# Pinning the transfers between two matrix products, and the last operand splits, to text order

## The chip, the cores and the metric

The kernel runs on one core of a Trainium2 chip. The metric is the device time of one execution in microseconds (us), the median of several runs. The engines named here are TensorE (PE, with its weight loads PEld), VectorE (DVE), ScalarE (ACT), GpSimd (POOL) and SyncE (SP), which here only issues DMA transfers; SPq is its queue.

## The reference

One layer of a streaming encoder, 1024 tokens of width 1024, float32. Only its end matters here:

```
x = x + concat(mixers) @ W_out                  # 1024 x 1024
h = rms_norm(x, mlp_norm_g)
f = square(relu(h @ W1))                        # 1024 -> 4096
x = x + f @ W2                                  # 4096 -> 1024
```

## The kernel before, in words

Every product is computed with operands split into a high part (rounded to the fast fp32r format) and a low remainder, so a product takes three matmuls (`mm3`): high x high, high x low, low x high. A split costs a cast on ACT and a subtraction on DVE. Weights are split by `w_split` into `whi` and `wlo`.

The two MLP products (FF1 with W1, FF2 with W2) are each done by a seven-product scheme on 2x2 blocks: instead of eight block products there are seven, numbered 1 to 7, on sums and differences of blocks. Those sums are made by POOL (`left`, `right`) and, for the activations x of FF1, in `x2_ready`. The work is a list of **units** of 12 matmuls of 128x512: ("1", p, i) is FF1, column block p (0 to 15), product i; ("2", c, i, n) is FF2, chunk c of p's, product i, n-th p of the chunk. `mlp(n)` issues the transfers of unit n, prepares (splits) the operands of unit n+2 and runs unit n. FF1's products are stored to DRAM by `f_store` as `f{p}_{i}` (seven tiles of 256 KB for each p) and read back by `load_f` for FF2. FF2's weights come by `load_w2` (two tiles of 512 KB for each p). The residual x, saved to `x2d` in DRAM by `x2_ready`, is loaded again (eight tiles of 512 KB) into slots that FF1 has finished with.

`x2_ready(dt)` runs behind the last output-projection matmuls of row block dt. It stores x2[dt] to DRAM, squares it for the norm, scales it in place by the norm weight on ACT, and makes the splits for products 1 and 5 (dt < 4) or 6, 2 and part of 7 (dt >= 4); `x2_late` then makes the rest of 7, and 4 and 3, in one go. Tiles of splits: P4 to P7 are product 6, P8 to P11 product 2, P12, P13, xh3, xl3 product 7, P0 to P3 product 4, xh0, xl0, P16, P17 product 3.

The order on each engine is not that of the text: a scheduler at build time sorts instructions by its own estimate of when their inputs are there. So a transfer whose slot is free early can go ahead of one that stands earlier in the text. Instructions of one engine then run in that order, each waiting for its inputs, and all DMA issues named here are in SP's one queue.

Of the kernel before, what the change touches and what calls it, by code (L numbers as in the profile page):

```python
# [29 lines left out]
V_MIX, V_MLP, V_GQ, V_GK, V_RET, V_PWA, V_PWG = 0, 8, 16, 17, 18, 22, 24  # L30
# [46 lines left out]
def build(tc, d):  # L77
    nc = tc.nc
# [8 lines left out]
    V, S, GP, TE = nc.vector, nc.scalar, nc.gpsimd, nc.tensor  # L87
    uid = [0]

    def nm(s):  # L90
        uid[0] += 1
        return f"{s}_{uid[0]}"

    def bank(tag):
        return pp.tile([P, 512], F32, tag=tag, name=nm(tag))

    def slot(tag, shape=(P, T), dt=F32):
        pool = xp if tag[0] == "x" else pg
# [57 lines left out]
    vec = cp.tile([P, V_N], F32, tag="vec", name="vec")  # L156
# [543 lines left out]
    x2, x2d = [], []  # L700
    for dt in range(NK):
        t = slot(X2S[dt])
# [12 lines left out]
          3: ("xh0", "xl0", "P16", "P17")}  # L715
    xr = {}

    def x_split(i, kk, src):
        t = slot(XS[i][kk], (P, 2, 512), F32R)
        S.copy(t[:, 0, :], src)  # L720
        V.tensor_tensor(out=t[:, 1, :], in0=src, in1=t[:, 0, :].bitcast(F32), op=ALU.subtract)
        xr[i, kk] = t

    sq2 = {}

    def x2_ready(dt):
        x = x2[dt]
        nc.sync.dma_start(x2d[dt], x)
        if dt == 0:
            sq = sq2[0] = pg.tile([P, T], F32, tag="glu0", name="sq2")  # L730
        else:
            sq = slot(("DM", "glu1")[dt % 2])
        S.activation(sq, x, AF.Square)
        S.activation(x, x, AF.Copy, scale=vec[:, V_MLP + dt:V_MLP + dt + 1])
        kk = dt % 4
        a, b = x[:, 0:512], x[:, 512:1024]
        if dt < 4:
            x_split(1, kk, a)
            GP.tensor_tensor(out=a, in0=b, in1=a, op=ALU.subtract)
            x_split(5, kk, a)  # L740
        else:
            t, b12 = x2[kk][:, 0:512], x2[kk][:, 512:1024]
            V.tensor_tensor(out=t, in0=b, in1=t, op=ALU.subtract)
            x_split(6, kk, t)
            x_split(2, kk, a)
            GP.tensor_tensor(out=b12, in0=b, in1=b12, op=ALU.subtract)
            if kk < 2:
                x_split(7, kk, b12)
            GP.tensor_tensor(out=t, in0=a, in1=t, op=ALU.subtract)
        if dt > 0:  # L750
            V.tensor_tensor(out=sq2[0], in0=sq2[0], in1=sq, op=ALU.add)

    def x2_late():
        for kk in range(2, 4):
            x_split(7, kk, x2[kk][:, 512:1024])
        for kk in range(4):
            x_split(4, kk, x2[kk][:, 0:512])
        for kk in range(4):
            x_split(3, kk, x2[kk + 4][:, 512:1024])
# [74 lines left out]

    def f_store(p, i, src):
        fd[p, i] = dp.tile([P, 512], F32, tag=f"f{p}_{i}", name=f"f{p}_{i}")
        nc.sync.dma_start(fd[p, i], src)

    def hidden(o, src, hf):
        V.scalar_tensor_tensor(out=o, in0=src, scalar=0.0, in1=rbc2[:, 512 * hf:512 * hf + 512], op0=ALU.max,  # L840
# [74 lines left out]
    def load_w2(p):  # L915
        raw2[p] = []
        for j in range(2):
            tag = WS2[nw2[0]]
            nw2[0] += 1
            t = wp.tile([P, 1024], F32, tag="wr", name=nm("wr"), bufs=4) if tag == "wr" else slot(tag)  # L920
            nc.sync.dma_start(t, d["w_ff2"][2 * p + j])
            raw2[p].append(t)

    fin = {}
# [1 line left out]
    def load_f(p, i):  # L926
        t = slot(FI[nfi[0] % len(FI)], (P, 512))
        nfi[0] += 1
        nc.sync.dma_start(t, fd[p, i])
        fin[p, i] = t  # L930

    def r_split(src):
# [20 lines left out]
    def run_ff2(c, i, n):  # L953
        s = {1: "X", 6: "X", 7: "X", 4: "X", 5: "Y", 3: "Y", 2: "Y"}[i]
        first = i in (1, 5, 2)
        if n == 0 and first:
            ps2[s] = [bank(t) for t in {"X": "ggtt", "Y": "zzoo"}[s]]
        wh, wl = opl.pop((c, i, n))
        fh, fl = opr.pop((c, i, n))
        last = n == len(chunks[c]) - 1  # L960
        for dt in range(4):
            cs = slice(dt * P, dt * P + P)
            mm3(ps2[s][dt], wh[:, cs], wl[:, cs], fh, fl, first and n == 0, last, not first)
        if not last:
            return
        rh, ch = {1: (0, 0), 2: (0, 0), 5: (1, 1), 7: (1, 1), 6: (0, 1), 3: (0, 1), 4: (1, 0)}[i]
        for dt in range(4):
            a = x2[4 * rh + dt][:, 512 * ch:512 * ch + 512]
            add(a, ps2[s][dt], a)
            if c == len(chunks) - 1 and i in (3, 7, 2, 4):  # L970
                r = (4 * rh + dt) * P
                nc.sync.dma_start(d["yT"][r:r + P, 512 * ch:512 * ch + 512], a)

    order1 = (1, 5, 6, 2, 7, 4, 3)
    units = [("1", 0, 1), ("1", 0, 5), ("1", 1, 1), ("1", 1, 5)]
# [2 lines left out]
    n1 = len(units)  # L978
# [8 lines left out]
    def f_upto(n):  # L987
        while nf[0] < min(n, len(f_order)):
            load_f(*f_order[nf[0]])
            nf[0] += 1  # L990

    def transfers(n):

        v = units[n + 2] if n + 2 < len(units) else None
        if v and v[0] == "1" and v[2] == 6 and v[1] + 2 < npair:
            load_w1(v[1] + 2)
        if n == n1 - 7:
            load_w2(0)
            load_w2(1)
            f_upto(3)  # L1000
        if n == n1 - 5:
            for dt in range(NK):
                x2[dt] = slot(C[dt])
                nc.sync.dma_start(x2[dt], x2d[dt])
        if n == n1 - 4:
            load_w2(2)
            f_upto(4)
        if n == n1 - 2:
            f_upto(6)
        if n >= n1:  # L1010
# [10 lines left out]
    def mlp(n):  # L1021
        transfers(n)
        if n + 2 < len(units):
            prep[units[n + 2][0]](*units[n + 2][1:])
        run[units[n][0]](*units[n][1:])

    for dt in range(NK):
# [49 lines left out]
```

## Time and profile before

| | |
|---|---|
| median of 3 runs | 1180.6 us (1180.12 to 1184.6) |
| profiled execution | 1179.3 us, of which the span of the profile is 1177.4 us |
| PE busy | 1131.6 us (96% of the span) |
| DVE, POOL, ACT busy | 867.1, 541.9, 489.8 us |

PE is busy nearly all the time, so what can be won lies in the few places where it stands still or runs at a lower clock. The page's second part gives 40 slices of 29.4 us each: the output projection ends and FF1 begins in slice 18 (counted from 0), FF2 begins in slices 28 and 29.

### The profile page before, as it was taken

The numbers are of one execution on the slowest core, as the hardware profiler recorded it, in microseconds if no ns is written. First come the engines' busy times: TensorE is split into PE (matmuls) and PEld (weight loads), VectorE is DVE, ScalarE is ACT, GpSimd is POOL, SyncE is SP. The second block draws the span as 40 slices with busy tenths as digits, with TensorE's granted clock in tenths as the row PEclk, the third lists the DMA queues.
The fourth block names the chain that finished last, engine by engine and source line by source line (L and its number), as shares of the span: only waits on it lengthen the run. The fifth ranks groups of instructions, "written<-read, shape, count | busy, mean of one in ns | idle before, by whom it ended". The sixth has DMA issues, their size and how long they took to land.

```text
span 1177.4 us, 17628 instructions
## 1 busy us (share of the span) xinstructions
PE 1131.6 (96%) x6376; PEld 984.6 (84%) x6376; DVE 867.1 (74%) x1347; ACT 489.8 (42%) x925; POOL 541.9 (46%) x440
## 2 busy tenths in 40 slices
PE   7999999999999999997999999999669999999998
PEld 6998889999999998786888888888458888888887
DVE  6787766769897887689765657574749797896964
ACT  7675644532323243555433333333324434444441
POOL 3565545346752553354555565647553250531400
PEclk9999999999999999998999999999889999999999
DMA  8111111021111151213444444453995346233332
GB/s 283 37 37 37 54 41 48 22 63 60 55 60 38 53 189 54 78 57 117 161 143 143 161 147 160 145 166 126 370 352 168 101 140 191 81 108 89 108 123 93
DMA packets 63734, 137.11 MB, mean 116 GB/s; under 512 B 7200, under 2 KB 11936, under 8 KB 63648
## 3 DMA queue, kind: packets, MB, share of 16 engines
q1 hardware_dynamic: 63072, 135.56, 35.0%
q8 instruction: 50, 0.82, 0.3%
q10 hardware_dynamic: 576, 0.44, 0.1%
q14 instruction: 36, 0.29, 0.1%
HBM read 98.22 MB, written 37.75 MB: 115 GB/s over the span
## 4 chain that ended last, share of the span: by engine, by line
PE 73%; DVE 12%; DMA 6%; issue 4%; POOL 2%; ACT 2%; SPq 0%; DVEq 0%; ACTq 0%; POOLq 0%
PE g L108 12%; PE g L110 11%; PE g L109 11%; PE t L108 4%; PE t L110 4%; PE t L109 4%; PE z L109 3%; PE z L110 3%; PE z L108 3%; PE o L108 3%; PE o L109 3%; PE o L110 3%; DVE wlo L153 3%; PE o L366 2%; PE t L347 1%
## 5 line engine op out<-in xcount | busy, mean ns | idle before, releaser
L153 DVE TENSOR_TENSOR wlo<-sum,whi 128x512 fp32r<-128x512 f32 x78 | 78.9, 1011 | 95.0 <-ACT whi L152 91.2
L153 POOL TENSOR_TENSOR wlo<-wraw,whi 128x512 fp32r<-128x512 f32 x57 | 86.2, 1527 | 78.0 <-ACT whi L152 75.5
L152 ACT CAST whi<-sum 128x512 fp32r<-128x512 f32 x78 | 48.1, 618 | 115.2 <-POOL sum L810 50.9
L153 DVE TENSOR_TENSOR wlo<-wr,whi 128x512 fp32r<-128x512 f32 x80 | 79.0, 993 | 12.1 <-ACT whi L152 12.1
L336 POOL TENSOR_TENSOR be<-be,kp 128x512 f32<-128x512 f32 (+3 forms) x48 | 46.0, 961 | 78.4 <-DVE kp L332 49.9
L152 ACT CAST whi<-wr 128x512 fp32r<-128x512 f32 x80 | 48.2, 619 | 56.0 <-PE g L109 16.8
L815 POOL TENSOR_TENSOR sum<-wr 128x512 f32<-128x512 f32 x16 | 24.5, 1529 | 101.5 <-DMA wr<-in_w_ff_dram 79.3
L152 ACT CAST whi<-wraw 128x512 fp32r<-128x512 f32 x68 | 41.8, 621 | 58.0 <-DMA wraw<-in_w_in_dram 21.8
L332 DVE TENSOR_TENSOR_SCAN kp<-kp 128x512 f32<-128x512 f32 (+3 forms) x48 | 51.1, 1066 | 10.6 <-ACT kp L325 10.1
L525 DVE SCALAR_TENSOR_TENSOR DM__508_2651<-glu,vec,DM__508_2651 128x512 f32<-128x512 f32 x60 | 53.9, 937 | 0.1
L167 POOL TENSOR_TENSOR rs<-ss,nhalf 128x4 f32<-128x4 f32 (+1 forms) x36 | 37.3, 1038 | 30.2 <-DVE ss L633 15.3
L525 DVE SCALAR_TENSOR_TENSOR glu<-glu,vec 128x512 f32<-128x512 f32 x60 | 47.5, 854 | 0.0
L810 POOL TENSOR_TENSOR sum<-wr,sum 128x512 f32<-128x512 f32 x19 | 32.0, 1684 | 7.5 <-DVE wlo L153 7.5
L325 ACT ACTIVATE kp<-z 128x512 f32<-128x512 f32 (+3 forms) x48 | 23.6, 494 | 16.7 <-PE z L322 13.0
L108 PE MATMUL g<-whi,xh__12_100 128*128 128x256 f32 x82 | 25.3, 309 | 2.8 <-DVE P__107_556 L300 0.9
L810 POOL TENSOR_TENSOR sum<-sum,wr 128x512 f32<-128x512 f32 x18 | 25.2, 1402 | 3.0 <-DVE wlo L153 3.0
L326 ACT ACTIVATE be<-z 128x512 f32<-128x512 f32 (+3 forms) x48 | 23.4, 493 | 4.9 <-PE t L347 4.9
L108 PE MATMUL g<-whi,xh__34_250 128*128 128x256 f32 x82 | 23.4, 285 | 1.7 <-ACT xh__34_250 L186 1.7
L110 PE MATMUL g<-whi,xl__53_362 128*128 128x256 f32 x82 | 23.3, 286 | 1.6 <-DVE xl__53_362 L187 1.6
L347 PE MATMUL t<-ident,be 128*128 128x128 f32 x144 | 24.2, 274 | 0.1
L110 PE MATMUL g<-whi,xl__46_323 128*128 128x256 f32 x82 | 23.4, 287 | 0.4 <-DVE xl__46_323 L187 0.4
L109 PE MATMUL g<-wlo,xh__52_361 128*128 128x256 f32 x82 | 23.5, 287 | 0.0
(2892 smaller groups left out, 4366.6 us busy)
## 6 DMA issues: line engine op xcount, KB each, us to landing
wr<-in_w_ff_dram SPq DMA_DIRECT2D x40, 512.0 KB, 3.9
wraw<-in_w_in_dram SPq DMA_DIRECT2D x52, 256.0 KB, 3.1
P__418_2109<-in_rot_dram SPq DMA_DIRECT2D x32, 128.0 KB, 2.1
wraw<-in_w_out_dram SPq DMA_DIRECT2D x16, 256.0 KB, 2.7
P__18_143<-in_xT_dram SPq DMA_DIRECT2D x1, 512.0 KB, 4.7
P__22_176<-in_xT_dram SPq DMA_DIRECT2D x1, 512.0 KB, 5.7
P__29_215<-in_xT_dram SPq DMA_DIRECT2D x1, 512.0 KB, 3.7
P__33_248<-in_xT_dram SPq DMA_DIRECT2D x1, 512.0 KB, 7.3
```

What stands on the lines that cost most here:

```text
L108: TE.matmul(out, lh, rh, start=start, stop=False, skip_group_check=on)
L109: TE.matmul(out, lh, rl, start=False, stop=False, skip_group_check=on)
L110: TE.matmul(out, ll, rh, start=False, stop=stop, skip_group_check=on)
L152: S.copy(hi, raw)
L153: (lo_engine or GP).tensor_tensor(out=lo, in0=raw, in1=hi.bitcast(F32), op=ALU.subtract)
L167: GP.tensor_tensor(out=out, in0=in_, in1=nhalf[:, 0:in_.shape[1]], op=ALU.pow)
L332: V.tensor_tensor_scan(rev, rev, rev, kp[:, n:n + 1], op0=ALU.mult, op1=ALU.bypass)
L336: GP.tensor_tensor(out=be[:, 0:n], in0=be[:, 0:n], in1=kp[:, 1:n + 1], op=ALU.mult)
L347: TE.transpose(pt[:, j * P:j * P + P], be[:, j * P:j * P + P], ident)
L525: V.scalar_tensor_tensor(out=acc, in0=src, scalar=vec[:, o:o + 1], in1=acc, op0=ALU.mult, op1=ALU.add)
L810: (eng or GP).tensor_tensor(out=o, in0=x, in1=y, op=ALU.subtract)
L815: GP.tensor_tensor(out=s, in0=a21, in1=a22, op=ALU.add)
```

## The change

Three parts. (1) From unit n1-7 on (n1 is the number of FF1 units; n1-7 is p = 15, product 1) every transfer of the MLP goes through `load`, which pins the DMA behind the instruction that stands before it in the text on SP's queue. The loads of x2 are done in two halves. (2) `x2_late` is cut in three: the rest of product 7 ahead of unit 4, product 4 ahead of unit 5, product 3 ahead of unit 6, each instruction pinned behind its engine's previous one in the text. (3) For dt >= 4 the norm weight g is no longer applied to x in place on ACT: it is folded into the splits (ACT's scale; a scalar_tensor_tensor on DVE), and eight subtractions move from POOL to DVE as scalar_tensor_tensor.

```
+    ordered = [False]
+    def load(out, in_):
+        i = nc.sync.dma_start(out, in_)
+        if ordered[0]:
+            tc.keep_in_program_order(i)
...
+    def x_split(i, kk, src, g=None, late=False):
         t = slot(XS[i][kk], (P, 2, 512), F32R)
...
+            ops = (S.activation(hi, src, AF.Copy, scale=g),
+                   V.scalar_tensor_tensor(out=lo, in0=src, scalar=g, in1=hi.bitcast(F32), op0=ALU.mult,
+                                          op1=ALU.subtract))
+        if late:
+            for o in ops:
+                tc.keep_in_program_order(o)
...
-        S.activation(sq, x, AF.Square)
-        S.activation(x, x, AF.Copy, scale=vec[:, V_MLP + dt:V_MLP + dt + 1])
...
         else:
-            V.tensor_tensor(out=t, in0=b, in1=t, op=ALU.subtract)
+            V.scalar_tensor_tensor(out=t, in0=b, scalar=g, in1=t, op0=ALU.mult, op1=ALU.subtract)
             x_split(6, kk, t)
-            x_split(2, kk, a)
-            GP.tensor_tensor(out=b12, in0=b, in1=b12, op=ALU.subtract)
+            x_split(2, kk, a, g)
+            V.scalar_tensor_tensor(out=b12, in0=b, scalar=g, in1=b12, op0=ALU.mult, op1=ALU.subtract)
             if kk < 2:
                 x_split(7, kk, b12)
-            GP.tensor_tensor(out=t, in0=a, in1=t, op=ALU.subtract)
+            S.activation(sq, x, AF.Square)
...
         if n == n1 - 7:
+            ordered[0] = True
             load_w2(0)
             load_w2(1)
             f_upto(3)
-        if n == n1 - 5:
-            for dt in range(NK):
+        if n in (n1 - 5, n1 - 3):
+            for dt in range(4) if n == n1 - 5 else range(4, NK):
                 x2[dt] = slot(C[dt])
-                nc.sync.dma_start(x2[dt], x2d[dt])
+                load(x2[dt], x2d[dt])
...
-    x2_late()
     for n in range(3, len(units)):
+        if n in (4, 5, 6):
+            x2_late({4: 7, 5: 4, 6: 3}[n])
```

What the built programs say, first on SP where FF2's transfers begin. Before, the stores of p = 14 and 15, the loads of f and the weights of FF2 for p = 4 to 9 (P12 on) stand mixed:

```order
L837 DMA f14_5_8722<-xh5__1450_8595 128x512
L921 DMA P0__1616_9390<-in_w_ff2_dram 128x1024
L837 DMA f14_7_8728<-xl5__1451_8596 128x512
L929 DMA xh4__1474_8741<-f0_1_6468 128x512
L837 DMA f15_1_8919<-xh6__1481_8767 128x512
L837 DMA f14_6_8725<-xh5__1450_8595 128x512
L921 DMA P12__1576_9195<-in_w_ff2_dram 128x1024
L921 DMA P1__1617_9392<-in_w_ff2_dram 128x1024
L837 DMA f14_4_8731<-xl5__1451_8596 128x512
L929 DMA xl4__1475_8743<-f1_1_6587 128x512
L921 DMA P13__1577_9197<-in_w_ff2_dram 128x1024
L921 DMA xh3__1594_9290<-in_w_ff2_dram 128x1024
```

In the changed program the last store of p = 14 comes first, then the weights of p = 0 and 1 (wr, wr, glu0, DM), then the f tiles of FF2's first three units, then half of x2:

```order
L101 DMA f14_4_8727<-xl5__1451_8592 128x512
L101 DMA wr_1470_8729<-in_w_ff2_dram 128x1024
L101 DMA wr_1471_8731<-in_w_ff2_dram 128x1024
L101 DMA glu0__1472_8733<-in_w_ff2_dram 128x1024
L101 DMA DM__1473_8735<-in_w_ff2_dram 128x1024
L101 DMA xh4__1474_8737<-f0_1_6464 128x512
L101 DMA xl4__1475_8739<-f1_1_6583 128x512
L101 DMA xh5__1476_8741<-f2_1_6747 128x512
L101 DMA xh1__1488_8784<-x2d0_5212 128x1024
L101 DMA xl1__1489_8786<-x2d1_5215 128x1024
L101 DMA xh2__1490_8788<-x2d2_5218 128x1024
L101 DMA xl2__1491_8790<-x2d3_5221 128x1024
```

Before the change the weights of p = 0 and 1 stood among the stores of p = 13 or further up, and x2 stood 14 to 24 rows ahead of f14_4, so both had been asked for by then. The next rows now are P4, P5 (weights of p = 2), f0_5, the other half of x2, f1_5, f2_5, the seven stores of p = 15 and f0_6, f1_6, f2_6.

A little further on SP. Before, nine weight tiles that FF2 needs only from chunk 1 on stand between the second (f1_1) and the third f tile (f2_1); these are the last seven of them, three stores and f2_1:

```order
L921 DMA xl3__1595_9292<-in_w_ff2_dram 128x1024
L921 DMA P2__1652_9557<-in_w_ff2_dram 128x1024
L921 DMA P3__1653_9559<-in_w_ff2_dram 128x1024
L921 DMA xh0__1676_9659<-in_w_ff2_dram 128x1024
L921 DMA xl0__1677_9661<-in_w_ff2_dram 128x1024
L921 DMA P16__1694_9755<-in_w_ff2_dram 128x1024
L921 DMA P17__1695_9757<-in_w_ff2_dram 128x1024
L837 DMA f15_3_8921<-xl6__1482_8768 128x512
L837 DMA f15_2_8923<-xl6__1482_8768 128x512
L837 DMA f15_5_8926<-xh7__1483_8769 128x512
L929 DMA xh5__1476_8745<-f2_1_6751 128x512
```

Now the same weight tiles stand one pair at a time between f loads, behind f2_2, f3_1 and so on:

```order
L101 DMA xl6__1557_9093<-f2_2_6751 128x512
L101 DMA wr_1558_9095<-in_w_ff2_dram 128x1024
L101 DMA wr_1559_9097<-in_w_ff2_dram 128x1024
L101 DMA xh7__1563_9119<-f0_4_6480 128x512
L101 DMA xl7__1567_9141<-f1_4_6599 128x512
L101 DMA xh4__1571_9167<-f2_4_6763 128x512
L101 DMA xl4__1575_9189<-f3_1_6911 128x512
L101 DMA P12__1576_9191<-in_w_ff2_dram 128x1024
L101 DMA P13__1577_9193<-in_w_ff2_dram 128x1024
```

So fourteen weight tiles that stood ahead of f0_6 before now stand behind it.

Last, DVE at the start of FF1. Before, six low-part subtractions of products 3 and 4 (xl0, xh0, P16, P1, P0, P2) stand ahead of the weights `wlo_1089` of unit ("1", 1, 6):

```order
L721 TENSOR_TENSOR xl0__1066_6316<-xl6__831_5225,xl0__1066_6316 128x512
L721 TENSOR_TENSOR xh0__1065_6313<-xh6__830_5222,xh0__1065_6313 128x512
L774 TENSOR_TENSOR xl7__833_5231<-o_1045_6236,xl7__833_5231 128x512
L721 TENSOR_TENSOR P16__1067_6319<-xh7__832_5228,P16__1067_6319 128x512
L721 TENSOR_TENSOR P1__1062_6304<-xl4__827_5213,P1__1062_6304 128x512
L721 TENSOR_TENSOR P0__1061_6301<-xh4__826_5210,P0__1061_6301 128x512
L153 TENSOR_TENSOR wlo_1084_6402<-sum1_1012_6060,whi_1083_6401 128x512
L721 TENSOR_TENSOR P2__1063_6307<-xh5__828_5216,P2__1063_6307 128x512
L153 TENSOR_TENSOR wlo_1089_6430<-sum1_1025_6125,whi_1088_6429 128x512
```

Now, from the last output tile (xl7, the residual add of the last row block) on:

```order
L795 TENSOR_TENSOR xl7__833_5231<-o_1045_6230,xl7__833_5231 128x512
L734 SCALAR_TENSOR_TENSOR xl0__1080_6387<-xl6__831_5225,vec_75,xl0__1080_6387 128x512
L734 SCALAR_TENSOR_TENSOR P16__1081_6390<-xh7__832_5228,vec_75,P16__1081_6390 128x512
L761 SCALAR_TENSOR_TENSOR xl5__829_5219<-xl7__833_5231,vec_75,xl5__829_5219 128x512
L764 SCALAR_TENSOR_TENSOR xl5__829_5219<-xl7__833_5231,vec_75,xl5__829_5219 128x512
L161 TENSOR_TENSOR wlo_1084_6398<-sum1_1012_6058,whi_1083_6397 128x512
L769 TENSOR_TENSOR sq2_5831<-sq2_5831,glu1__1046_6248 128x1024
L734 SCALAR_TENSOR_TENSOR P17__1082_6393<-xl7__833_5231,vec_75,P17__1082_6393 128x512
L161 TENSOR_TENSOR wlo_1089_6426<-sum1_1025_6121,whi_1088_6425 128x512
L731 TENSOR_TENSOR P7__1047_6250<-xl5__829_5219,P7__1047_6250 128x512
L731 TENSOR_TENSOR xl3__1063_6307<-xl5__829_5219,xl3__1063_6307 128x512
```

Product 4's work on DVE has moved behind `wlo_1089` (its first instruction stands sixteen rows behind xl7), and two scalar_tensor_tensor on xl5 stand where P0, P1 and P2 stood.

## Rows read from the trace of the kernel before

**Rows 1.** The page, parts 1 and 2: PE busy, granted clock, traffic by slice.
```profile
PE 1131.6 (96%) x6376; PEld 984.6 (84%) x6376; DVE 867.1 (74%) x1347; ACT 489.8 (42%) x925; POOL 541.9 (46%) x440
PE   7999999999999999997999999999669999999998
PEclk9999999999999999998999999999889999999999
```
**Rows 2.** Waits of PE, the longest: who was waited for, us in total, times, longest.
```profile
PE g L108 <- ACT P__1512_8878 L935: 8.8, 1, 8.8
```
**Rows 3.** Timeline of PE, start of FF1: start, duration, [idle before, releaser].
```profile
533.61 0.39 PE L110 MATMUL o<-P__963_5772,wlo 128*128 128x512 f32 x1
...
540.56 0.50 PE L108 MATMUL t<-P__1009_6048,whi 128*128 128x512 f32 x1 [1.12 <-ACT whi L152]
...
546.73 0.80 PE L110 MATMUL t<-P__1009_6048,wlo 128*128 128x512 f32 x1 [5.43 <-DVE wlo L153]
547.32 0.63 PE L108 MATMUL t<-P__1022_6113,whi 128*128 128x512 f32 x1
547.75 0.63 PE L109 MATMUL t<-P__1022_6113,whi 128*128 128x512 f32 x1
```
**Rows 4.** Timeline of DVE, the same stretch.
```profile
541.45 1.75 DVE L721 TENSOR_TENSOR P__1062_6304<-xl__827_5213,P__1062_6304 128x512 fp32r<-128x512 f32 x1
543.12 1.74 DVE L721 TENSOR_TENSOR P__1061_6301<-xh__826_5210,P__1061_6301 128x512 fp32r<-128x512 f32 x1
...
546.00 0.68 DVE L153 TENSOR_TENSOR wlo<-sum,whi 128x512 fp32r<-128x512 f32 x1
```
**Rows 5.** Timeline of POOL: FF1's start, and the last tile of p = 14.
```profile
541.12 1.53 POOL L815 TENSOR_TENSOR sum<-wr 128x512 f32<-128x512 f32 x1 [2.54 <-DMA wr<-in_w_ff_dram]
...
838.63 1.29 POOL L810 TENSOR_TENSOR xl__1451_8596<-xl__1449_8594,xh__1450_8595 128x512 f32<-128x512 f32 x1
```
**Rows 6.** Timeline of ACT: the scaling of x2[7] in place.
```profile
544.25 1.15 ACT L734 ACTIVATE xl__833_5231<-xl__833_5231,vec 128x1024 f32<-128x1024 f32 x1 [2.23 <-DMA x2d<-xl__833_5231]
```
**Rows 7.** One scalar_tensor_tensor form on DVE: duration in ns, min/median/max.
```profile
L840 DVE SCALAR_TENSOR_TENSOR xl__1115_6630<-xl__1115_6630,rbc x2: 676/676/676, 596.8 to 597.4; 128x512 f32<-128x512 f32 x2
```
**Rows 8.** Timeline of PE: FF1's end, then FF2's units 1, 2, 3, 7, 8.
```profile
844.99 0.39 PE L110 MATMUL z<-P__1068_6322,wlo 128*128 128x512 f32 x1
854.13 1.22 PE L108 MATMUL g<-P__1512_8878,whi 128*128 128x512 f32 x2 [8.76 <-ACT P__1512_8878 L935]
...
860.41 0.73 PE L108 MATMUL g<-P__1516_8901,whi 128*128 128x512 f32 x2 [1.58 <-ACT P__1516_8901 L935]
...
870.81 1.22 PE L108 MATMUL g<-P__1525_8953,whi 128*128 128x512 f32 x2 [6.24 <-ACT P__1525_8953 L935]
...
883.69 0.39 PE L108 MATMUL g<-P__1552_9056,whi 128*128 128x512 f32 x1
...
886.41 0.39 PE L108 MATMUL g<-P__1556_9078,whi 128*128 128x512 f32 x1
```
**Rows 9.** Stretches of 5 us: busy of PE, PEld, DVE, ACT, POOL; PEclk, DMA share, GB/s.
```profile
840.00:845.00 5.00, 3.40 (x16) 2.50 (x14) 2.65 (x5) 1.33 (x3) 0.00 (x0) 1.00 1.02 417
...
850.00:855.00 5.00, 0.87 (x2) 0.77 (x3) 3.79 (x5) 1.77 (x3) 4.37 (x4) 0.50 1.04 417
...
865.00:870.00 5.00, 0.00 (x0) 0.00 (x0) 1.29 (x2) 0.57 (x2) 1.64 (x1) 0.80 1.04 402
```
**Rows 10.** Timeline of SP's queue: the issues of f0_1, f14_4, f2_1, f0_5.
```profile
843.64 0.32 SPq L929 DMA_DIRECT2D xh__1474_8741<-f  x1
...
848.60 0.33 SPq L837 DMA_DIRECT2D f<-xl__1451_8596  x1
...
862.51 0.32 SPq L929 DMA_DIRECT2D xh__1476_8745<-f  x1
...
868.94 0.32 SPq L929 DMA_DIRECT2D xl__1502_8828<-f  x1
```
**Rows 11.** DMA issues of one kind: count, KB each, median us to landing.
```profile
wr<-in_w_ff_dram SPq DMA_DIRECT2D x40, 512.0 KB, 3.9
```

More of the change, by code (lines that the diff above doesn't have):

```diff
@@ L716, in build @@
     xr = {}
-    def x_split(i, kk, src):
+    def x_split(i, kk, src, g=None, late=False):
         t = slot(XS[i][kk], (P, 2, 512), F32R)
-        S.copy(t[:, 0, :], src)
-        V.tensor_tensor(out=t[:, 1, :], in0=src, in1=t[:, 0, :].bitcast(F32), op=ALU.subtract)
+        hi, lo = t[:, 0, :], t[:, 1, :]
+        if g is None:
+            ops = S.copy(hi, src), V.tensor_tensor(out=lo, in0=src, in1=hi.bitcast(F32), op=ALU.subtract)
+        else:
+            ops = (S.activation(hi, src, AF.Copy, scale=g),
[4 more added lines that the diff above has]
+                tc.keep_in_program_order(o)
         xr[i, kk] = t
     sq2 = {}
+    gs = [vec[:, V_MLP + dt:V_MLP + dt + 1] for dt in range(NK)]
     def x2_ready(dt):
-        x = x2[dt]
+        x, g = x2[dt], gs[dt]
         nc.sync.dma_start(x2d[dt], x)
@@ L737, in x2_ready @@
         if dt < 4:
+            S.activation(sq, x, AF.Square)
+            S.activation(x, x, AF.Copy, scale=g)
             x_split(1, kk, a)
@@ L742, in x2_ready, with x2_late @@
             t, b12 = x2[kk][:, 0:512], x2[kk][:, 512:1024]
-            V.tensor_tensor(out=t, in0=b, in1=t, op=ALU.subtract)
+            V.scalar_tensor_tensor(out=t, in0=b, scalar=g, in1=t, op0=ALU.mult, op1=ALU.subtract)
             x_split(6, kk, t)
-            x_split(2, kk, a)
-            GP.tensor_tensor(out=b12, in0=b, in1=b12, op=ALU.subtract)
+            x_split(2, kk, a, g)
+            V.scalar_tensor_tensor(out=b12, in0=b, scalar=g, in1=b12, op0=ALU.mult, op1=ALU.subtract)
             if kk < 2:
                 x_split(7, kk, b12)
-            GP.tensor_tensor(out=t, in0=a, in1=t, op=ALU.subtract)
+            S.activation(sq, x, AF.Square)
         if dt > 0:
             V.tensor_tensor(out=sq2[0], in0=sq2[0], in1=sq, op=ALU.add)
[L753 to L759, printed above, removed]
+    def x2_late(i):
+        for kk in range(2 if i == 7 else 0, 4):
+            t = x2[kk][:, 0:512]
+            if i == 4:
+                tc.keep_in_program_order(V.scalar_tensor_tensor(out=t, in0=x2[kk + 4][:, 0:512], scalar=gs[kk + 4], in1=t,
+                                                                op0=ALU.mult, op1=ALU.subtract))
+            if i == 3:
+                x_split(i, kk, x2[kk + 4][:, 512:1024], gs[kk + 4], late=True)
+            else:
+                x_split(i, kk, t if i == 4 else x2[kk][:, 512:1024], late=True)
     EARLY = 3
@@ L836, in f_store @@
         fd[p, i] = dp.tile([P, 512], F32, tag=f"f{p}_{i}", name=f"f{p}_{i}")
-        nc.sync.dma_start(fd[p, i], src)
+        load(fd[p, i], src)
     def hidden(o, src, hf):
@@ L920, in load_w2 @@
             t = wp.tile([P, 1024], F32, tag="wr", name=nm("wr"), bufs=4) if tag == "wr" else slot(tag)
-            nc.sync.dma_start(t, d["w_ff2"][2 * p + j])
+            load(t, d["w_ff2"][2 * p + j])
             raw2[p].append(t)
@@ L928, in load_f @@
         nfi[0] += 1
-        nc.sync.dma_start(t, fd[p, i])
+        load(t, fd[p, i])
         fin[p, i] = t
@@ L971, in run_ff2 @@
                 r = (4 * rh + dt) * P
-                nc.sync.dma_start(d["yT"][r:r + P, 512 * ch:512 * ch + 512], a)
+                load(d["yT"][r:r + P, 512 * ch:512 * ch + 512], a)
     order1 = (1, 5, 6, 2, 7, 4, 3)
```

## The prediction

> **What bounds the kernel now.** I read the page first. PE is busy for 96% of the span, so only stretches in which it stands still or runs slowly can give time back. The 40 slices show two such places around the change: slice 18 (the start of FF1) and above all slices 28 and 29 (the end of FF1 and the start of FF2), where PE's digit falls to 6 and the granted clock to 8 [rows 1]. PE's waits, sorted by the longest, lead to the same place: one wait of 8.8 us for a cast of a loaded f tile [rows 2]. Then I read PE's timeline at both places.
>
> At the start of FF1 PE waits 1.12 us and then 5.43 us for `wlo`, the low part of the weights of unit ("1", 1, 6); behind the long wait its matmuls start 0.43 us apart (547.32, 547.75) [rows 3]. Undisturbed they start 0.227 us apart: a unit of 12 takes 886.41 − 883.69 = 2.72 us [rows 8]. About eight matmuls go at the slow pace, 8 × 0.2 = 1.6 us. The place loses 1.12 + 5.43 + 1.6 = 8.2 us. DVE's timeline says why: it makes that `wlo` only at 546.00, with P1 and P0 ahead of it at 1.75 and 1.74 us each [rows 4]. POOL was at work at that moment (1.53 us from 541.12) [rows 5], and `wlo` itself, the same shape, took 0.68 us [rows 4]; so I put some 1.1 us of each long one down to the collision. In the same stretch ACT can scale x2[7] only once its store to DRAM has been read out, a wait of 2.23 us and then 1.15 us of scaling [rows 6].
>
> At the start of FF2, FF1's last matmul starts at 844.99. The units of FF2 then start at 854.13 (idle 8.76), 860.41 (idle 1.58) and 870.81 (idle 6.24), and unit 7 only at 883.69 [rows 8]. Meanwhile the DMA engines are full: 417, 417 and 402 GB/s, a DMA share over 1 [rows 9]. So PE waits for transfers, and what matters is which transfer is served first. SP's queue shows it: f2_1, which unit 3 needs, is issued at 862.51, f0_5 at 868.94 [rows 10]. By the order, fourteen weight tiles, 14 × 0.524 = 7.3 MB that chunk 0 doesn't use, go ahead of f0_6. The clock makes it worse: PEclk is 0.50 in the stretch 850 to 855 [rows 9], and unit 1 took 860.41 − 1.58 − 854.13 = 4.70 us instead of 2.72 [rows 8].
>
> **The change, part by part.** *FF2's transfers in text order.* The weights of p = 0 to 2 and the eight x2 tiles now stand behind f14_4, the last store of p = 14; before, the weights of p = 0 and 1 and x2 had been asked for earlier. So the change adds to the refill as much as it takes away, and I add it up by arrival. POOL's result for f14_4 is there at 838.63 + 1.29 = 839.9, yet SP issued the store at 848.60, since other rows stood ahead [rows 5, 10]. Pinned, it goes at 840.0 and the first weight tile at 840.4. A tile of 512 KB lands 3.9 us after its issue [rows 11], at 844.3. From there each 512 KB costs 0.524 MB / 0.41 MB per us = 1.28 us and each 256 KB 0.64 us, at the rate that the stretches show [rows 9]. Down the new list: three more weight tiles and f0_1 land by 848.8, with a cast of some 0.6 us unit 1 starts at 849.4; f1_1, f2_1, four x2 tiles and P4 land by 856.4, unit 3 starts at 857.0 (unit 2 is over by then, even if unit 1 takes 4.70); P5 and f0_5 by 858.3, so unit 4 follows unit 3 at 859.7; four more x2 tiles and f1_5 by 864.1, unit 5 at 864.7; f2_5 and the seven stores of p = 15 by 869.2, f0_6 by 869.8, unit 7 at 870.4. Check: 14 × 0.524 + 14 × 0.262 = 11.0 MB by 0.41 is 26.8 us, from 843.0 to 869.8. If the clock falls in the idle time ahead of unit 5 and it takes 4.70, unit 7 comes at 864.7 + 4.70 + 2.72 = 872.1; I take half of that delay, 0.9. Unit 7 at 871.3 instead of 883.69 is **12.4 us**. Bounds: the rates 417 and 402 move 869.8 by 0.5; with no idle time from unit 1 on, unit 7 stands at 849.4 + 6 × 2.72 = 865.7 (18 us, not to be had while f0_6 lands at 869.8, so 13.3 is the upper end); a refill that starts only at 848.60, as f14_4 went before, comes 8.6 later and leaves 3.8.
>
> Pinning costs nothing on SP itself: an issue is 0.32 us [rows 10], and what stands behind a waiting one is what FF2 needs next. A pinned load whose slot isn't free would hold all behind it: the x2 slots belong to products 1 and 5 of p = 15, done early in p = 15's seven units, and xh6 (f0_6) waits for the store f15_1, seven places further up, which goes out during the refill anyway. The weights put back are next needed in chunk 1, 21 units × 2.72 = 57 us after unit 1, and the queue is empty again by then.
>
> The Trainium skill bears on the rate: its page "DMA: Bandwidth & Descriptors", section "Where 436 GB/s comes from", says that for transfers between HBM and SBUF the HBM side binds, at about 358 GB/s. By it the refill would take 11.0 / 0.358 = 30.7 us, 3.9 later, and the kernel some 1166 us; the stretches show 402 to 417 [rows 9], so the sum keeps to these.
>
> *Late splits and folded norm weights.* Behind the last output tile DVE now has, up to and with `wlo_1089`: the add into xl7, two splits of product 3, two on xl5, wlo_1084, the add into sq2, a third split, wlo_1089. Eight at 0.6 us from start to start, as the two scalar_tensor_tensor at 596.8 and 597.4 [rows 7], and one of double length, 1.2: 6.0 us. The last output matmul starts at 533.61 [rows 3]; in the new order three matmuls less stand ahead of it, so 532.9, and its result is there at 533.3. 533.3 + 6.0 = 539.3; I add two collisions with POOL of 1.1, as at P1 and P0 [rows 4]: 541.5, and P7 behind it at 542.1. PE's new order puts 31 matmuls between that output matmul and P7: 533.2 + 31 × 0.227 = 540.2, and `wlo_1089` three later. So PE waits some 1.9 us for P7 instead, and no longer for `wlo_1089`; after an idle time of 1.58 unit 2 of FF2 ran without a fall of the clock [rows 8], so I add none. The gain is 8.2 − 1.9 = **6.3 us**. Bounds: no wait is 8.2; four more collisions (4.4 us) leave 1.9.
>
> What is added: eight subtractions move from POOL to DVE, 8 × 0.6 = 4.8 us; four of them (dt 4 to 7, on the second halves) and four of product 4, which now run behind `wlo_1089`. DVE's next due tile is P0, some 45 matmuls behind P7, 10 us, with eleven instructions of DVE ahead of it, about 7.5 us: a cover of 2.5 us. Without it the 4.8 us would be PE's. The scaling by ACT goes, 1.15 us each [rows 6]; the casts that take its place are there anyway, so I cost it at nothing beyond the wait, which is in the 6.3.
>
> **Sum.** Profiled execution 1179.3 − 6.3 − 12.4 = 1160.6. The median of the runs is 1180.6, 1.3 above it, so the forecast is **1162 us**.
>
> **Rivals.** *A. The refill starts no earlier.* Something that I don't see holds f14_4 or the first weight tile to 848.6. For it: that is when the store went before [rows 10]. Against: the rows ahead of it are gone. FF2's gain is 3.8 and the time 1162 + 8.6 = 1170.6.
>
> *B. DVE becomes the bound at FF1's start.* It takes eight more instructions there and collides with POOL when W1's sums are made [rows 4, 5]. Then the wait moves to P7 and P0 and the first gain falls to between 1.9 and −3: 1166 to 1171.
>
> *C. No difference.* A and B together: 1180.6 − 3.8 − 0 = 1176.8, within 0.5% (5.9 us, about what a measurement of this kernel can tell from no change).
>
> *D. Slower.* Weights and x2, once asked for early, now stand in one piece with FF2's first units. If the refill of 11.0 MB is much slower than the rows say, FF2 starts later than before. To come out above 1186.5 with FF1's gain kept, unit 7 would have to start 12.2 later than 883.69, at 895.9: less 1.5 for clock and cast, 11.0 MB from 843.0 to 894.4, that is 214 GB/s. The stretches show twice that [rows 9].
>
> **How the numbers follow.** Forecast 0.60, its own range 1156 to 1168 (its bounds 13.3 and 8.2 at one end, one more late arrival at the other); A 0.16, B 0.11, C 0.08, D 0.05. The range takes in A and B up to 1173 and at the lower end two more us than the bounds, 1154. Faster by over 0.5% (below 1174.7): 0.60 + 0.16 + 0.11 = 0.87; within 0.5%: 0.08; slower: 0.05.
>
> **What would show it.** In the new profile PE's wait for `wlo` at some 541 is gone and one of about 2 us for P7 has taken its place; the stretch 540 to 550 has a PEclk near 1. f14_4 is issued within a microsecond of POOL's result, FF2's unit 1 starts some 4.4 us behind FF1's last matmul and unit 7 some 26 (38.7 before [rows 8]), with the DMA rate above 400 GB/s between them. The prediction is wrong if SP stands waiting at a pinned load with the DMA engines idle, if DVE shows more than two instructions over 1.7 us ahead of `wlo_1089`, or if P0 to P3 become PE's new wait.

## The result and the profile after

The changed kernel takes 1164.18 us (median of 4 runs, 1163.4 to 1164.32) against 1180.36 us (4 runs): ratio 0.9854, 95% interval 0.9831 to 0.9878. It is faster by 1.5%, as forecast (1162, range 1154 to 1173). The profiled execution takes 1164.28 us with a span of 1162.5, so the span is 14.9 us shorter. It was run once more on another chip, where it gave 0.9837 (0.9820 to 0.9854). The kernel before runs at 1179 to 1185 us, and the longer of these runs have the lower mean granted clock (0.982 against 0.990 in the profiled one), so every version below is compared with the kernel before on its own chip, by the ratio.

The page's parts 1 and 2, as in [rows 1]: the low digits of slice 18 are gone, and of slices 28 and 29 (6 and 6 before) 8 and 7 are left.

```profile
PE 1132.3 (97%) x6376; PEld 986.6 (85%) x6376; DVE 871.3 (75%) x1355; ACT 487.5 (42%) x921; POOL 530.5 (46%) x432
...
PE   7999999999999999999999999999879999999998
...
PEclk9999999999999999999999999999989999999999
```

**The start of FF1.** PE's timeline answers to [rows 3] (start, duration, in brackets the idle time before and who ended it). Neither of the two waits is left; the longest is 0.24 us. P__1047 is P7, the tile that the prediction has PE wait for.

```profile
540.42 0.39 PE L116 MATMUL t<-P__1047_6250,whi 128*128 128x512 f32 x1
541.05 1.95 PE L224 MATMUL o<-ones,sq 128*128 128x1 f32 x16 [0.24 <-DVE sq L769]
...
543.41 0.39 PE L118 MATMUL t<-P__1009_6046,wlo 128*128 128x512 f32 x1
...
544.88 0.63 PE L117 MATMUL t<-P__1039_6186,whi 128*128 128x512 f32 x1
545.30 0.63 PE L118 MATMUL t<-P__1039_6186,wlo 128*128 128x512 f32 x1
```

DVE's timeline, answering to [rows 4]: the two scalar_tensor_tensor on xl5 take 1.8 us each (1.80, 1.78) beside POOL's sums (1.49 us from 535.52, 1.62 us from 537.09), and the `wlo` that PE needs at 543.41 begins at 541.58.

```profile
535.76 1.80 DVE L761 SCALAR_TENSOR_TENSOR xl__829_5219<-xl__833_5231,vec,xl__829_5219 128x512 f32<-128x512 f32 x1
537.48 1.78 DVE L764 SCALAR_TENSOR_TENSOR xl__829_5219<-xl__833_5231,vec,xl__829_5219 128x512 f32<-128x512 f32 x1
...
541.58 0.68 DVE L161 TENSOR_TENSOR wlo<-sum,whi 128x512 fp32r<-128x512 f32 x1
```

**The start of FF2.** PE's timeline, answering to [rows 8]: FF1's last matmul, then the first matmuls of units 1, 3, 4, 5 (with its second wait), 6 and 7 (P__1539 is unit 5's f tile split in two, P__1552 unit 7's).

```profile
836.05 0.39 PE L118 MATMUL z<-P__1082_6393,wlo 128*128 128x512 f32 x1
840.45 0.74 PE L116 MATMUL g<-P__1512_8874,whi 128*128 128x512 f32 x2 [4.01 <-ACT P__1512_8874 L956]
...
848.28 0.50 PE L116 MATMUL g<-P__1525_8949,whi 128*128 128x512 f32 x1
...
851.14 0.61 PE L116 MATMUL z<-P__1534_8976,whi 128*128 128x512 f32 x2
...
858.47 1.22 PE L116 MATMUL z<-P__1539_8999,whi 128*128 128x512 f32 x2 [3.35 <-ACT P__1539_8999 L956]
...
861.81 0.79 PE L117 MATMUL z<-P__1539_8999,whi 128*128 128x512 f32 x1 [1.27 <-DVE P__1539_8999 L957]
...
865.24 0.63 PE L116 MATMUL z<-P__1544_9026,whi 128*128 128x512 f32 x2
...
869.22 0.74 PE L116 MATMUL g<-P__1552_9052,whi 128*128 128x512 f32 x2 [1.06 <-ACT P__1552_9052 L956]
```

Counted from FF1's last matmul, forecast and measurement agree to 0.4 us up to unit 4 and part at unit 5 (the last column is an experiment below):

| us behind FF1's last matmul | before | forecast | after | first9_pinned |
|---|---|---|---|---|
| unit 1 (f0_1) | 9.1 | 4.4 | 4.4 | 4.6 |
| unit 3 (f2_1) | 25.8 | 12.0 | 12.2 | 13.0 |
| unit 4 (f0_5) | | 14.7 | 15.1 | 17.6 |
| unit 5 (f1_5) | | 19.7 | 22.4 | 20.4 |
| unit 7 (f0_6) | 38.7 | 26.3 | 33.2 | 26.5 |

The 14.9 us come in three pieces. FF1's last matmul starts at 836.05 instead of 844.99, 8.94 us earlier. Some 7.4 of these are FF1's start: matmul by matmul, the two traces agree to 0.01 us at 522.7 and stand 7.38 us apart all through FF1, from 569 to 818. The other 1.5 are for the most part a wait at p = 14 that I had not counted: before the change PE stood idle there for 1.26 us, waiting for a low part that DVE made late, and no longer does.

```profile
817.35 1.29 POOL L810 TENSOR_TENSOR glu__1472_8737<-glu__1472_8737 128x512 f32<-128x512 f32 x1
...
828.25 0.50 PE L108 MATMUL z<-xh__1065_6313,whi 128*128 128x512 f32 x1 [1.26 <-DVE xl__1449_8594 L844]
```

The first of these two lines of the kernel before is the last of four sums, from 813.61 on, that POOL made there for FF2's first weights, ahead of its work on the f tiles. The traces that show the wait (of before, of `splits_only` and of `weights_early` below) are those in which POOL makes these four sums so early. `early_first9` and `early_prep_pinned` ask for the same weights as early, make the sums later and don't have it. So the wait goes with the place of the sums, not with the early transfers.

Unit 8 starts at 872.51 instead of 886.41, 13.9 earlier, so FF2's start adds 5.0 (5.5 at unit 7's first matmul; unit 7 itself then took 3.29 us instead of 2.72). The last 1.0 is spread over later chunks.

Where do the 7 us go between unit 4 and unit 7? SP's queue, answering to [rows 10], shows the issues of f14_4, f1_5 and f0_6:

```profile
829.94 0.32 SPq L101 DMA_DIRECT2D f<-xl__1451_8592  x1
...
846.29 0.32 SPq L101 DMA_DIRECT2D P__1508_8866<-f  x1
...
856.79 0.32 SPq L101 DMA_DIRECT2D xh__1517_8933<-f  x1
```

and the DMA table of the stretch 830 to 872 (as [rows 11]: count, KB each, us to landing) when the two f tiles land, at 846.3 + 9.1 = 855.4 and 856.8 + 4.4 = 861.2:

```profile
P__1508_8866<-f SPq DMA_DIRECT2D x1, 256.0 KB, 9.1
...
xh__1517_8933<-f SPq DMA_DIRECT2D x1, 256.0 KB, 4.4
```

ACT's timeline shows when they are cast: at 857.80 and 868.55, 2.4 and 7.4 us after they had landed. ACT, which works in order, stood idle at casts of weight sums ahead of each: one waited 2.52 us for POOL's sum, two others 4.56 and 2.15 us for a buffer that PE had not yet given back.

```profile
857.27 0.62 ACT L160 CAST whi<-sum 128x512 fp32r<-128x512 f32 x1 [2.52 <-POOL sum L831]
857.80 0.61 ACT L956 CAST P__1539_8999<-P__1508_8866 128x512 fp32r<-128x512 f32 x1
...
865.26 0.62 ACT L160 CAST whi<-sum 128x512 fp32r<-128x512 f32 x1 [4.56 <-PE o L117]
...
868.02 0.62 ACT L160 CAST whi<-sum 128x512 fp32r<-128x512 f32 x1 [2.15 <-PE o L117]
868.55 0.61 ACT L956 CAST P__1552_9052<-xh__1517_8933 128x512 fp32r<-128x512 f32 x1
```

### The profile page after: what moved, and what is told of

Its sections match the earlier page's. It is cut to its first block, busy times and chain, and to the rows that moved or that the text cites. A ratio compares the mean times of both kernels' runs of the same rounds, so it can differ in the third digit from the quotient of the medians.

```text
span 1162.5 us, 17630 instructions
## 1 busy us (share of the span) xinstructions
PE 1132.3 (97%) x6376; PEld 986.6 (85%) x6376; DVE 871.3 (75%) x1355; ACT 487.5 (42%) x921; POOL 530.5 (46%) x432
## 4 chain that ended last, share of the span: by engine, by line
PE 84%; DVE 9%; DMA 3%; issue 2%; ACT 1%; SPq 0%; POOL 0%; DVEq 0%; ACTq 0%; POOLq 0%
PE g L116 12%; PE g L118 12%; PE g L117 12%; PE t L117 5%; PE t L118 5%; PE t L116 5%; PE o L117 5%; PE o L116 5%; PE o L118 4%; PE z L117 4%; PE z L118 4%; PE z L116 4%; DVE DM__508_2651 L533 3%; PE o L374 2%; PE t L355 1%
## 5 line engine op out<-in xcount | busy, mean ns | idle before, releaser
L161 DVE TENSOR_TENSOR wlo<-sum,whi 128x512 fp32r<-128x512 f32 x78 | 75.5, 971 | 84.5 <-ACT whi L160 84.5
L161 DVE TENSOR_TENSOR wlo<-wr,whi 128x512 fp32r<-128x512 f32 x80 | 76.6, 963 | 10.0 <-ACT whi L160 9.0
```

The lines of the kernel that those rows point to most:

```text
L161: (lo_engine or GP).tensor_tensor(out=lo, in0=raw, in1=hi.bitcast(F32), op=ALU.subtract)
```

## The experiments

**The two parts alone.** `pins_only` has the pinned transfers with `x_split`, `x2_ready` and `x2_late` of before; `splits_only` has the rest of the change and pins no transfer:

```
 pins_only
-        if n in (4, 5, 6):
-            x2_late({4: 7, 5: 4, 6: 3}[n])
+    x2_late()
     for n in range(3, len(units)):
...
 splits_only
-            ordered[0] = True
```

> The transfers pinned to text order alone; splits and norm weights as before the change. If the two parts work in separate places, the gain of FF1's start (7.4 us between the two traces) is missing: 1164.2 + 7.4 = 1171.6 us, PE's wait of some 5.4 us for wlo is back at the start of FF1, and FF2's first units stand to each other as in the changed kernel. If the new order of the transfers needs the new splits, or the other way round, the time lies elsewhere: above 1174 or below 1169.

> Late splits and folded norm weights alone; no transfer is pinned (x2 still in two halves). Separate places: 1180.4 - 7.4 = 1173 us, with no long wait at FF1's start and FF2's start as before the change (idle 8.8 and 6.2 us). If the missing wait at p = 14 (1.4 us) is also a fruit of the splits, 1171.5.

On their chip the kernel before took 1183.99 us. `pins_only`: 1176.17, ratio 0.9930 (0.9910 to 0.9949). `splits_only`: 1171.67, 0.9898 (0.9883 to 0.9912). The two savings, 0.7% and 1.0%, add up to 1.7%, within the uncertainty of the 1.5 to 1.6% of both together, as parts that work in separate places would. In us both expectations were worked out for a kernel before of 1180.4: as a ratio 1171.6 is 0.9925, which `pins_only` meets, while `splits_only` gained more than its 1173 or 1171.5 (0.9937, 0.9925). Its span is 8.4 us shorter than that of the traced kernel before; where the rest of its 1.0% lies no trace shows. PE's timelines show the separate places. In `pins_only` the wait at FF1's start is there again and FF2 starts like the changed kernel. (FF1's start costs 3.9 us more in this trace than in that of before: its matmuls go on 0.43 us apart until 559.4, there only until 550, and the granted clock is 0.50 in these windows.)

```profile
547.25 0.79 PE L118 MATMUL t<-P__1009_6048,wlo 128*128 128x512 f32 x1 [5.45 <-DVE wlo L161]
...
851.89 1.22 PE L116 MATMUL g<-P__1512_8878,whi 128*128 128x512 f32 x2 [3.96 <-ACT P__1512_8878 L943]
...
869.89 0.74 PE L116 MATMUL z<-P__1539_9003,whi 128*128 128x512 f32 x2 [3.35 <-ACT P__1539_9003 L943]
```

In `splits_only` FF2's long waits are those of before, and the wait at p = 14 is there too (1.05 us):

```profile
844.56 1.22 PE L116 MATMUL g<-P__1512_8874,whi 128*128 128x512 f32 x2 [8.31 <-ACT P__1512_8874 L956]
...
861.84 1.22 PE L116 MATMUL g<-P__1525_8949,whi 128*128 128x512 f32 x2 [6.50 <-ACT P__1525_8949 L956]
```

**Inside FF1's start.** `fold_only` keeps the folded norm weights and makes the late splits in one go, unpinned:

```
-        if n in (4, 5, 6):
-            x2_late({4: 7, 5: 4, 6: 3}[n])
+    x2_late()
     for n in range(3, len(units)):
```

The four subtractions of product 4 go back into `x2_ready` with them, still on DVE. `late_only` keeps the three pinned pieces, but ACT scales x in place and POOL makes the eight subtractions, as before:

```
+        S.activation(x, x, AF.Copy, scale=vec[:, V_MLP + dt:V_MLP + dt + 1])
...
-            V.scalar_tensor_tensor(out=b12, in0=b, scalar=g, in1=b12, op0=ALU.mult, op1=ALU.subtract)
+            GP.tensor_tensor(out=b12, in0=b, in1=b12, op=ALU.subtract)
```

> The changed kernel with norm weights folded, but the late splits in one go and not pinned, as before the change. If the order of the late splits ahead of wlo is what cost at FF1's start, the wait for wlo comes back in part: two collisions and six splits ahead of it, PE waits 3 to 5 us, ratio 0.988 to 0.990. If the norm weight's wait for the store to DRAM was the cause, nothing comes back: 0.985 to 0.986.

> The changed kernel with the late splits cut in three and pinned, but the norm weight applied in place by ACT and the eight subtractions on POOL as before. If the order of the late splits was the cause, most of FF1's gain stays: 0.985 to 0.988. If the wait for the store was the cause, PE waits 4 us or more for P7 or wlo: 0.989 to 0.991.

On their chip the kernel before took 1181.46 us. `fold_only`: 1168.41, 0.9880 (0.9856 to 0.9904). `late_only`: 1171.97, 0.9913 (0.9886 to 0.9940). By the ratios `fold_only` comes out at the edge of what was expected for the order (0.988 to 0.990; PE waits 2.32 us and not 3 to 5), `late_only` a little above what was expected for the store. Counted in the traces matmul by matmul, from ahead of FF1's start to its middle, `fold_only` loses 3.8 and `late_only` 6.0 of the 7.4 us: folding alone brings 3.6, the pinned pieces alone 1.4, and the rest comes only with both. In `late_only` `wlo` comes late and PE waits 3.64 us:

```profile
545.25 0.79 PE L118 MATMUL t<-P__1009_6048,wlo 128*128 128x512 f32 x1 [3.64 <-DVE wlo L161]
```

One link ahead of that `wlo` is the store of x2[6]: ACT waits for it before it can scale in place, DVE's subtraction waits for the scaling, and the add into the last output tile, which in the changed kernel follows its matmul (533.17) at 533.84, comes 6.5 us behind its matmul (534.05).

```profile
532.95 1.15 ACT L752 ACTIVATE xh__832_5228<-xh__832_5228,vec 128x1024 f32<-128x1024 f32 x1 [2.16 <-DMA x2d<-xh__832_5228]
...
534.14 0.69 DVE L761 TENSOR_TENSOR xh__828_5216<-xh__832_5228,xh__828_5216 128x512 f32<-128x512 f32 x1 [0.89 <-ACT xh__832_5228 L752]
...
540.57 0.68 DVE L789 TENSOR_TENSOR xl__833_5231<-o,xl__833_5231 128x512 f32<-128x512 f32 x1
```

The other link is POOL: two of DVE's splits in that stretch take 1.41 and 1.78 us beside the subtractions that POOL makes there. Since `late_only` brings back both the scaling in place and the subtractions on POOL, it doesn't tell one from the other; no run has only one of them.

In `fold_only` three of DVE's splits for product 4 (P1, P0, P2) are back ahead of the add into sq2, and PE waits 2.32 us for it:

```profile
543.04 3.57 PE L224 MATMUL o<-ones,sq 128*128 128x1 f32 x16 [2.32 <-DVE sq L770]
```

By the traces the fold as a whole was the larger cause and the order of the splits the smaller; the intervals of the two ratios overlap, so the sizes stay rough.

**Are POOL's sums the new bound at FF2's start?** `sums_on_dve` lets DVE make six of them:

```
-        opl[c, i, n] = w_split(left(a, i, sums2.get(p)), V)
+        opl[c, i, n] = w_split(left(a, i, sums2.get(p), V if c == 0 and i in (5, 6) else None), V)
```

> The changed kernel, with the six weight sums of products 5 and 6 of FF2's first three p made by DVE instead of POOL. Theory: in the changed kernel the f tiles of units 5 to 7 lie in SBUF 2 to 7 us before they are cast, because ACT's casts stand in order behind casts of sums that POOL makes at 1.7 us each beside a busy DVE; then the waits of 3.4 and 1.3 us and the half clock behind them go, about 5 us: 1159 us. Rival (the transfers still bound FF2's start): no gain, 1164, or up to 1168 since DVE gets six instructions more.

1163.29 us, 0.9825 (0.9810 to 0.9839), which can't be told from the 0.9837 and 0.9854 of the changed kernel. Nor does the trace show a gain at the place: this one is 1.12 us ahead of the changed kernel already in the middle of FF1, which the edit doesn't touch, and only 0.64 ahead behind FF2's start, which so lost 0.5. The wait for unit 5's low part went from 1.27 to 3.84 us:

```profile
854.81 0.73 PE L116 MATMUL z<-P__1539_8999,whi 128*128 128x512 f32 x2 [1.00 <-ACT P__1539_8999 L956]
...
859.85 0.80 PE L117 MATMUL z<-P__1539_8999,whi 128*128 128x512 f32 x1 [3.84 <-DVE P__1539_8999 L957]
```

My theory in this form fell: it isn't the speed of POOL. The cast does come earlier (854.14), but DVE now makes product 6's sums and low parts ahead of the f tile's. What stayed possible is the order.

**Order.** `prep_pinned` pins the preparation of chunk 0 (sums, casts, low parts) to text order, which prepares unit by unit; `first9_pinned` does so only for the first nine units, products 1, 5 and 6:

```
+        if pin:
+            for o in ops:
+                tc.keep_in_program_order(o)
...
+        pinned[0] = c == 0 and i in (1, 5, 6)
-        opl[c, i, n] = w_split(left(a, i, sums2.get(p)), V)
-        opr[c, i, n] = r_split(fin.pop((p, i)))
+        opl[c, i, n] = w_split(left(a, i, sums2.get(p)), V, pinned[0])
+        opr[c, i, n] = r_split(fin.pop((p, i)), pinned[0])
```

> The changed kernel, with the preparation of FF2's first 21 units (sums on POOL, casts on ACT, low parts on DVE) pinned to text order too, so that an f tile's cast and low part stand ahead of product 6's and product 7's weights. Theory (order of preparation is what costs): the f tile of unit 5 is cast when it lands, some 2.4 us earlier, its low part 3 us earlier, the waits of 3.4 and 1.3 us at 858 shrink to under 2 in all and the half clock behind them goes: ratio to the kernel before 0.981 to 0.983 (changed kernel 0.9854). Rival (POOL's and DVE's work in that stretch is too much in any order): 0.985 to 0.986. Rival (transfers): no change.

> As prep_pinned, but only the preparation of FF2's first nine units (products 1, 5 and 6) is pinned; the rest of chunk 0 is left to the scheduler. In prep_pinned FF2's start gained some 7 us and 4.6 us were lost again at the end of chunk 0, where PE waited 2.9 us for DVE's add into x2. If the pins of the later units caused that loss, it goes: 1164.2 - 7 = 1157 us or less on a chip where the kernel before takes 1180.4, ratio 0.979 to 0.980 less 0.003, that is 0.976. If the loss belongs to a faster start (work that is due earlier than it can be made), it stays: 0.980.

`prep_pinned`: 1159.01 us against 1181.46, 0.9797 (0.9772 to 0.9821). `first9_pinned`: 1158.85 against 1183.72, 0.9789 (0.9770 to 0.9807), where the unaltered changed kernel gave 0.9837 on the same chip:

> The changed kernel once more, unaltered, for comparison with the two on the same chip: 0.9854 within 0.0025. In some runs of kernels that share its start of FF1, eight or so matmuls at 544 to 550 ran at half clock and in others not, which is worth some 1.6 us.

The interval of `first9_pinned` lies below that of the changed kernel on the same chip (0.9820 to 0.9854); `prep_pinned` came out a little better than its 0.981 to 0.983. In `first9_pinned` PE's waits for the casts of units 5 and 7 are gone (0.39 and 0.91 us are left for their low parts); in `prep_pinned` 0.70 us is left at unit 5. ACT's timeline of `first9_pinned` shows what the casts wait for now: the f tiles themselves.

```profile
853.67 0.62 ACT L964 CAST P__1539_8999<-P__1508_8866 128x512 fp32r<-128x512 f32 x1 [4.72 <-DMA P__1508_8866<-f]
...
859.41 0.62 ACT L964 CAST P__1552_9052<-xh__1517_8933 128x512 fp32r<-128x512 f32 x1 [3.56 <-DMA xh__1517_8933<-f]
```

Unit 7 starts 26.5 us behind FF1's last matmul: the 26.3 of the forecast. Behind FF2's start `prep_pinned` stands 8.2 us ahead of the changed kernel and at the end only 3.9. It gave 4.3 us back at the end of chunk 0, where PE waited for DVE's add into x2:

```profile
905.39 0.47 PE L116 MATMUL g<-P__1624_9415,whi 128*128 128x512 f32 x1 [2.87 <-DVE P__1501_8836 L873]
```

In `first9_pinned` that wait is gone, and it stays 7.9 us ahead of the changed kernel from unit 8 to the end. So the pins of the later units had caused the loss. Of the 7.9 us 1.9 stand in FF1 already, where the edit changes nothing; 6.0 are FF2's start. The total misses its expectation (0.976, below the interval): on the same chip the medians differ by 5.2 us. The runs of `first9_pinned` spread from 1156.39, the profiled one, to 1159.86, and why the others are slower the one trace doesn't show. By the medians it is not faster than `prep_pinned`; only the traces tell the two apart.

**A smaller refill.** `weights_early` asks for the weights of p = 0 and 1 early, as before the change; `early_first9` and `early_prep_pinned` add this to the pinned preparation.

```
-            ordered[0] = True
             load_w2(0)
             load_w2(1)
+            ordered[0] = True
```

> The changed kernel, with the weights of p = 0 and 1 asked for early as before the change (not pinned) and all other transfers pinned. 2.1 MB less stand ahead of f0_1, 5.1 us at 0.41 MB per us, and POOL can make the sums of p = 0 and 1 before FF1 ends. If transfers bound FF2's start, unit 1 starts some 4 us and unit 7 some 5 us earlier: 1159 us. If POOL's sums bound it, unit 1 starts 4 us earlier, but the sums of product 6 and p = 2 remain, and units 5 to 7 gain 2 to 4 us: 1160 to 1162.

> Both of the above: weights of p = 0 and 1 asked for early, and the preparation of FF2's first 21 units pinned to text order. If order of preparation and the size of the refill cost apart from each other, the gains add: 0.9806 less 0.003, that is 0.977 to 0.979. If both only take away the same wait, 0.980 to 0.981.

> first9_pinned, and the weights of p = 0 and 1 asked for early. If the loss at the end of chunk 0 goes here too (1.7 us in early_prep_pinned), 0.978 less 0.0015 = 0.9765. The early weights cost some 1.4 us in p = 14, so they are worth less than 2 us beside first9_pinned; the two may be equal.

`weights_early`: 1161.32 us, 0.9806 (0.9789 to 0.9822). `early_prep_pinned`: 1156.45, 0.9780 (0.9755 to 0.9804). `early_first9`: 1155.81, 0.9767 (0.9751 to 0.9783), the fastest version of all, 0.7% below the changed kernel on the same chip. The last two came out as expected for gains that add, but the interval of the first of them takes in the rival's 0.980 too. By the medians the early weights bring some 3 us beside either pinned preparation; the intervals of the pairs overlap, so that is not shown. With the early weights alone FF2's start gains some 3 us in the trace and the wait at p = 14 takes 1.3 back. The casts still stand in the old order, and unit 5 waits for its low part:

```profile
859.18 0.79 PE L117 MATMUL z<-P__1539_8999,whi 128*128 128x512 f32 x1 [3.43 <-DVE P__1539_8999 L957]
```

## Why the prediction was right, and where it was not

*FF1's start* (6.3 forecast, 7.4 measured). The count of DVE's work was right to 0.8 us: `wlo_1089` was to be done at 541.5 and was done at 542.26, 0.5 of the delay because the chain began later (533.84 for 533.3); the two collisions came as counted (1.80 and 1.78 us). The step that failed is the wait of 1.9 us for P7. P7's first matmul at 540.42 takes the high part alone, which ACT had cast at 537.60; I let it wait for DVE's low part, which PE needed only at 545.73. And PE had 16 narrow matmuls (541.05) to do before it came to `wlo` at 543.41. Instead eight matmuls then ran 0.43 us apart (from 544.45 on), which I had not counted and which cost some 1.5 us. With the short waits the place still loses 2.1 us, summed over PE's matmuls, of 9.4 before (8.2 in the prediction). So what was left came near the forecast 1.9 for another reason, and that is luck. As for the cause, I named the collisions, the order of the splits and the scaling in place without telling them apart; the traces put more on the fold as a whole than on the order. The scaling that I read in [rows 6], of x2[7], stands behind the cast for `wlo_1089` (539.89) and did not hold it; the one of x2[6] stands ahead, with a wait of 2.26 us for its store (532.64, in the same trace).

*FF2's start* (12.4 forecast; 5.0 measured, and 1.5 at p = 14). The transfers came as worked out: f1_5 landed 19.3 us behind FF1's last matmul (forecast 864.1 − 844.99 = 19.1), f0_6 25.1 (24.8). So the size of the refill, its rate and the issue of f14_4 were right. Stretches of the changed kernel (columns as in [rows 9]) reach 404 and 409 GB/s. The Trainium skill ("DMA: Bandwidth & Descriptors", section "Where 436 GB/s comes from") has the HBM side bind at about 358 GB/s for transfers between HBM and SBUF. These traces don't agree with it, and the measurement decides.

```profile
835.00:840.00 5.00, 1.44 (x7) 0.86 (x5) 3.54 (x5) 2.24 (x5) 3.50 (x3) 1.00 1.03 404
840.00:845.00 5.00, 4.20 (x11) 2.89 (x12) 4.57 (x3) 1.64 (x3) 5.00 (x4) 0.66 1.03 409
```

The step that failed is "with a cast of some 0.6 us unit 1 starts", carried on to units 5 and 7. It holds only while the cast is the next thing that ACT does. I had read SP's new order and left the order on ACT, DVE and POOL out: the weights of units 7 to 9 stand ahead of unit 5's f tile on ACT. Unit 7 came 33.2 − 26.3 = 6.9 us late: 2.7 for the late cast of unit 5, 1.3 for its low part, some 1.9 for the lower clock behind these waits (0.82 and 0.50 granted in 855 to 865) beyond the 0.9 that I had allowed, and 1.1 for unit 7's own cast. `first9_pinned`, which changes that order alone, gave 6.7 of it back at unit 7's start and 6.0 at unit 8's.

*The sum.* The profiled execution was forecast at 1160.6 and took 1164.3, 3.7 more. FF2's 12.4 were too much by 7.4; FF1's start brought 1.1 more, p = 14 1.5 and the later chunks 1.0 that I did not forecast; 7.4 − 1.1 − 1.5 − 1.0 makes 3.8, the same but for rounding. So the forecast came near partly by errors of opposite sign, which is luck too. One sum of the prediction is wrong in itself: the bounds 13.3 and 8.2 give 1180.6 − 21.5 = 1159.1 as the lower end of its own range, not 1156.

*The rivals.* A (refill starts late) is refuted by f14_4's issue at 829.94, within 0.1 us of POOL's result. B (DVE becomes the bound at FF1's start) is refuted by the lack of any long wait there, and C (no difference), which needed A and B together, falls with them. D (slow refill) is refuted by the rates.

*The signs.* No wait for P0 to P3 came, unit 1 starts 4.4 us behind FF1's last matmul, and exactly two instructions of DVE over 1.7 us stand ahead of `wlo_1089`, as said. Three signs did not come: the wait of 2 us for P7, a granted clock near 1 in 540 to 550 (it is 0.92 and 0.74), and unit 7 at some 26 us (33.2).

## What to carry to other kernels

When a transfer is moved ahead, read the order on the engines behind it too: a tile that lands early gains nothing while its cast stands behind other work in an in-order engine. Pinning one queue to text order while the engines that consume from it follow a scheduler's estimate leaves both out of step; pin the consumers at that place too, and no further than the place reaches. And an operation that waits for a store of its own operand (the scaling in place) can hold what stands behind it even if the engine that does it has time to spare; folding it into the next operation paid here, though only together with eight subtractions moved from POOL to DVE, and what each is worth alone no run shows.

## What was not expected of the hardware

Behind the 16 narrow matmuls (128x1) at FF1's start six wide ones ran at the normal pace in the trace of the changed kernel, and then eight 0.43 us apart (544.45 to 547.43), though PE had been idle for only 0.24 us before the narrow ones. Of the nine traces that share this start of FF1 four show it (the changed kernel both times, `weights_early`, `early_prep_pinned`) and five do not (`splits_only`, `sums_on_dve`, `prep_pinned`, `first9_pinned`, `early_first9`). The windows 545 to 550 of the changed kernel and of `sums_on_dve` (columns as in [rows 9]; the granted clock is 0.74 and 1.00):

```profile
545.00:550.00 5.00, 5.00 (x18) 4.02 (x17) 3.15 (x6) 1.80 (x3) 1.82 (x2) 0.74 0.31 105
```
```profile
545.00:550.00 5.00, 5.00 (x21) 3.61 (x21) 2.89 (x5) 1.55 (x3) 2.08 (x2) 1.00 0.35 105
```

It is worth some 1.5 us. No kernel was traced both with it and without it, so whether the run or the kernel decides stays open, and the 1.5 us stand in the comparisons of the changed kernel with the pinned ones above. For comparisons of single traces it means that the offset ahead of the place of interest has to be taken off first.
